# Sixteen expert buffers, the overflow branch behind the last gate and up products, and unpermuted token rows with strided gather columns

## The chip, the cores and the metric

The kernel runs on one core of a Trainium2 chip. The metric is the time of one execution on the device, in microseconds (us). [...] The engines are named as in the views: PE is TensorE's matmul and PEld its weight load, DVE is VectorE, ACT is ScalarE, POOL is GpSimd, SP is SyncE, which here issues nearly all loads.

## The reference, cut to what matters

256 tokens of width 1024 go through two blocks. The change touches only the end of the second one, a mixture of sixteen experts behind a two-level router, and the last norm:

```python
h2_l = modulate(rmsnorm(x_lat, norm2_g[l]), sh2, sc2)
x_lat = x_lat + g2 * hier_moe(h2_l, w_router_group[l], b_router_group[l], w_router_expert[l],
                              b_router_expert[l], w_exp_gate[l], w_exp_up[l], w_exp_down[l])
...
return rmsnorm(x_lat, final_g)

def hier_moe(h, w_rg, b_rg, w_re, b_re, w1, w3, w2):
    ...
    top_v, top_i = lax.top_k(le_g, TOP_K_IN_GROUP)
    w_top = jax.nn.softmax(top_v, axis=-1) * w_grp
    ...
    def expert_step(acc, xs):
        w1e, w3e, w2e, ge = xs
        y = (jax.nn.silu(t @ w1e) * (t @ w3e)) @ w2e
        return acc + ge[:, None] * y, None

    acc, _ = lax.scan(expert_step, jnp.zeros_like(t), (w1, w3, w2, gates))
```

Each token is given two of the four experts of one group. `w1` and `w3` (gate and up) are 1024x512 for each expert and `w2` (down) is 512x1024, all float32: 6 MiB an expert, 96 MiB in all.

## The kernel before

The blocks ahead of the experts take the time up to about 917 us. Then:

**Router.** For each half b of the tokens (128 rows) `x_add(b)` completes the residual `x[b]`, `x_turn(b)` transposes it, `logits(b)` and `pick(b)` give each token its two experts and its rank among the tokens of an expert. `x_high` (ACT, L1707) and `x_low` (DVE, L1711) write the normalized rows as a rounded part and the rest, `xnh` and `xnl` (the tiles H0 to H3). They permute the 1024 columns as they do so (`rows4`, `tiles4`), so that each block of 128 columns in H holds every fourth column of a half of x: this is the order in which a load of expert weights lays its rows on the partitions. The order of these steps on DVE and ACT is that of the code (`route`, a stretch with a manual schedule).

**Slots.** Each expert has 64 slots. `one_hot(b, e0, n)` (DVE, L1772) makes the 0/1 matrix from tokens to slots, first for experts 0 to 3, then for 4 to 15. `gather(p)` (L1788), once for every two pairs of experts, multiplies: for each of eight column blocks k four matmuls (high and low part, two halves of the tokens) with a block of H as the stationary operand, 256 slots as the moving one. The result, half a PSUM bank, is scaled and shifted by DVE into `xe` (L1800). Two consecutive k share a bank. `places()` sums the gates and counts the tokens that found no slot (`novi`).

**Experts.** Two experts form a pair, and TensorE works on both halves of its columns at once (`pair_mm`, 64 columns each). For p = 0 to 7 the program order of TensorE is: `gate(p)`; `down(p-1)` (for p = 0 `places()`); `up(p)`; `gather(p+1)` when p is odd and under 7; `back(p)`, the transposed one-hot; the `add` of pair p-1, which multiplies the slots back into token rows (`scatter`, L1877); `hidden_T(p)`, which transposes the hidden values. Behind the loop come `down(7)`, `scatter(7)` and the last norm (L2015 to L2035).

**Loads.** Each product needs four loads of 1 MiB, 128 partitions by 2048 values, 96 in all. `load_rows` (L235) issues them on SP in program order and takes the buffers in turn from three pools: five `rawa`, four `raw` (these serve the blocks ahead as well), four `rawb`. A load waits until the buffer's last reader is done; SP holds the loads behind it back. So the first thirteen loads (all of gate 0, up 0 and gate 1, and one of down 0) go out ahead of the experts, as their pools' memory comes free.

**Overflow.** Tokens beyond 64 for an expert are treated by a slow path inside `tc.If(nov > 0)` (L1904), in which all engines take part; it isn't taken with this data. Each engine reads `novi` and branches. The branch stands behind `hidden_T(6)`. The loads for `gate(7)`, `down(6)` and `up(7)` are issued in front of it, those for `down(7)` behind it. `down` takes its eight steps (f, n), four blocks f of the hidden columns and two halves n of the output, with f outermost; for p = 7 they are sorted by n, so that the first accumulator is done half-way.

## Time and profile before

| | |
|---|---|
| median of three runs | 1183.94 us (1183.94, 1177.48, 1184.63) |
| the profiled execution's own time | 1180.25 us |
| its span in the trace | 1178.5 us |
| mean granted clock of TensorE | 0.979 |
| PE busy | 1108.8 us (94%) |
| DVE / ACT / POOL busy | 621.2 / 477.3 / 60.7 us |
| instructions | 17991 |

The rows further down come from that one execution; their times are us from the start of its span. "idle before <-" in brackets is the time in which the engine had nothing to do ahead of a row, and the instruction that ended it. A matmul of float32 shows as two records. PEq and SPq are the queues of an engine in which branches, semaphores and DMA issues stand. A DMA share around 1.0 means that the sixteen DMA engines had no pause.

### The profile page before, as it was taken

To read this page: it belongs to the slowest core of one execution; us is meant where nothing else is said; L and a number is where in the kernel's file an instruction comes from. 1 tells how busy PE (TensorE), PEld (TensorE's weight loads), DVE (VectorE), ACT (ScalarE), POOL (GpSimd) and SP (SyncE) were. 2 spreads that over 40 slices of the span, in tenths; PEclk is the share of its full clock that TensorE was granted. 3 is DMA by queue.
4 is the path that set the end of the run, shared out by engine and by line. 5 is a ranking of instruction groups with operands and counts; after the bars stand their busy time and mean duration, and the time that the engine had idled before them with its cause. 6 is when DMAs were issued, how large, how long until landed. Compare 5 with 4: busy or idle time off the path is not lost. (4 is left out here: it accounts for less than half of the span.)

```text
span 1178.5 us, 17991 instructions
## 1 busy us (share of the span) xinstructions
PE 1108.8 (94%) x7527; PEld 870.1 (74%) x7527; DVE 621.2 (53%) x928; ACT 477.3 (40%) x711; POOL 60.7 (5%) x106
## 2 busy tenths in 40 slices
PE   6999999998988999999999999999899799999976
PEld 6999997887756888999998688888898534343432
DVE  4545545556976556455445865666656603232314
ACT  5444444476643355444444445555544300100002
POOL 1000001000330001000000100000000200000000
PEclk9999999999988999999999999999999799999988
DMA  9855654453557548555556454214285399999984
GB/s 338 275 191 179 198 180 158 157 169 112 179 197 261 197 139 304 195 179 185 175 191 218 153 179 160 72 55 152 96 327 210 145 366 419 421 420 420 421 354 175
DMA packets 119538, 262.98 MB, mean 223 GB/s; under 512 B 6873, under 2 KB 83802, under 8 KB 105242
## 3 DMA queue, kind: packets, MB, share of 16 engines
q1 hardware_dynamic: 118506, 258.88, 60.7%
q0 software_dynamic: 656, 2.36, 0.6%
q8 instruction: 61, 1.00, 0.3%
q10 hardware_dynamic: 288, 0.52, 0.1%
q14 instruction: 27, 0.22, 0.1%
HBM read 260.70 MB, written 1.05 MB: 222 GB/s over the span
## 5 line engine op out<-in xcount | busy, mean ns | idle before, releaser
L263 DVE TENSOR_TENSOR lo<-raw,hi 128x1024 fp32r<-128x1024 f32 x243 | 297.2, 1224 | 285.9 <-ACT hi L262 285.5
L262 ACT ACTIVATE hi<-raw 128x1024 fp32r<-128x1024 f32 x246 | 260.6, 1060 | 318.2 <-PE pj L227 203.3
L227 PE MATMUL pj<-H,hi 128*128 128x256 f32 x752 | 212.4, 283 | 4.1 <-issue 4.1
L226 PE MATMUL pj<-H,hi 128*128 128x256 f32 x752 | 216.2, 288 | 0.0
L228 PE MATMUL pj<-H,lo 128*128 128x256 f32 x752 | 212.4, 282 | 0.4 <-POOL lo L263 0.4
L226 PEld LDWEIGHTS pj<-H,hi 128*128 128x128 f32 x752 | 142.8, 190 | 8.5 <-issue 4.5
L228 PEld LDWEIGHTS pj<-H,lo 128*128 128x128 f32 x752 | 143.0, 190 | 5.2 <-issue 4.5
L227 PEld LDWEIGHTS pj<-H,hi 128*128 128x128 f32 x752 | 142.7, 190 | 1.3 <-issue 0.5
L228 PE MATMUL pj<-hTh,lo 128*128 128x256 f32 x352 | 99.4, 283 | 0.1
L227 PE MATMUL pj<-hTl,hi 128*128 128x256 f32 x352 | 99.2, 283 | 0.0
L226 PE MATMUL pj<-hTh,hi 128*128 128x256 f32 x352 | 99.1, 283 | 0.0
L227 PEld LDWEIGHTS pj<-hTl,hi 128*128 128x128 f32 x352 | 67.3, 192 | 1.3 <-DVE hTl L509 0.8
L226 PEld LDWEIGHTS pj<-hTh,hi 128*128 128x128 f32 x352 | 67.2, 192 | 1.2 <-ACT hTh L508 0.8
L228 PEld LDWEIGHTS pj<-hTh,lo 128*128 128x128 f32 x352 | 67.4, 192 | 0.3 <-DVE lo L263 0.3
L1881 DVE TENSOR_TENSOR yf<-yacc,K 128x512 f32<-128x512 f32 x16 | 11.0, 691 | 104.7 <-PE yacc L1832 82.5
L404 PE MATMUL acc<-lo,hTh 128*128 128x512 f32 x160 | 63.1, 394 | 0.0
L403 PE MATMUL acc<-hi,hTh 128*128 128x512 f32 x160 | 62.7, 392 | 0.0
L407 PE MATMUL acc<-hi,hTl 128*128 128x512 f32 x160 | 49.9, 393 | 0.0
L1832 PE MATMUL pu<-rawa,xe 128*64 128x512 f32 x160 | 45.3, 605 | 0.0
L1864 ACT ACTIVATE hT<-eT 128x512 f32<-128x512 f32 x8 | 4.8, 597 | 91.6 <-PE eT L1863 91.6
L1832 PE MATMUL pg<-raw,xe 128*64 128x512 f32 x128 | 35.8, 595 | 0.0
L1832 PE MATMUL yacc<-rawb,hT 128*64 128x512 f32 x128 | 35.5, 592 | 0.0
(496 smaller groups left out, 1895.2 us busy)
## 6 DMA issues: line engine op xcount, KB each, us to landing
raw<-in_w_in_dram SPq DMA_DIRECT2D x43, 1024.0 KB, 5.1
raw<-in_ffn_up_dram SPq DMA_DIRECT2D x22, 1024.0 KB, 5.2
raw<-in_ffn_down_dram SPq DMA_DIRECT2D x22, 1024.0 KB, 4.9
raw<-in_ffn_gate_dram SPq DMA_DIRECT2D x21, 1024.0 KB, 5.2
rawa<-in_w_exp_up_dram SPq DMA_DIRECT2D x20, 1024.0 KB, 19.2
raw<-in_w_exp_gate_dram SPq DMA_DIRECT2D x16, 1024.0 KB, 14.1
rawb<-in_w_exp_down_dram SPq DMA_DIRECT2D x16, 1024.0 KB, 17.5
raw<-in_w_mod_dram SPq DMA_DIRECT2D x15, 1024.0 KB, 5.0
```

What stands on the lines that cost most here:

```text
L226: mm(o, l[0], r[0], start=first, stop=False)
L227: mm(o, l[0], r[1], start=False, stop=False)
L228: mm(o, l[1], r[0], start=False, stop=last)
L262: ACT.activation(hi, r, AF.Copy)
L263: low = lambda: (sub or DVE).tensor_tensor(lo, r, f32(hi), op=OP.subtract)
L403: mm(ps[b][n], hh, wh[:, s_], start=first and f == 0, stop=False)
L404: mm(ps[b][n], hh, wl[:, s_], start=False, stop=False)
L407: mm(ps[b][n], ll, wh[:, s_], start=False, stop=last and f == 1)
L1832: mm(o[halves[u]], l[:, 64 * u:64 * u + 64], r[u], start=first, stop=last, tile_position=(0, 64 * u))
L1864: ACT.activation(t, ps, AF.Copy)
L1881: tt(part(yf, n), yaccs[p][n], part(g2b, n), op=OP.mult)
```

## The change

Seven things are edited together.

- **Buffers.** The expert loads take sixteen buffers in turn: five `rawa`, one that is made of the constant tiles K0 and K1 (now one tile K01), four `raw`, six `rawb`. To make room, the pool "moe" keeps two instead of four general tiles and one `xe` instead of two; `yf` of the scatter lives in K2; the gain of the residual (`g1b`) gets a tile of its own; final_g is loaded into K0 at the end, and the last norm uses K1 and the `xe` tile.
- **Rows.** `x_high` and `x_low` no longer permute; each is one operation on 128x1024. The permutation moves into `gather`, whose stationary operand is now every fourth column of H (a step of 16 bytes).
- **Gather.** The even k are evacuated by DVE, the odd ones by ACT. The first gather takes four banks at once, and both one-hots for experts 4 to 15 stand behind it.
- **Router.** PE joins the manual schedule of `route`.
- **Branch.** It stands behind `hidden_T(7)`; all loads, those of `down(7)` too, are issued in front of it.
- **Last product.** `down(7)` takes f = 0 and 1 for both halves n, then f = 2, 3 of the first half, then of the second.
- **Slow path.** Its loads go to ACT's queue; its tiles change with the pools.

```diff
@@ -98,7 +98,7 @@
     ffn={"4": 16, "2": 11, "1": 2, "m": 12},
     mid={"r4": 9, "r2": 6, "r1": 7, "rm": 16, "v4": 3, "s4": 6, "sm": 6, "gm": 4, "m2": 2, "mm": 2, "pm": 4, "cm": 4, "c1": 2},
     blk={"4": 9, "2": 5, "1": 7, "m": 25}, att={"4": 6, "2": 9},
-    moe={"4": 4, "xe": 2, "oh": 2, "h": 3, "1": 2, "m": 16}, raws=(5, 4, 4))
+    moe={"4": 2, "xe": 1, "oh": 2, "h": 3, "1": 2, "m": 16}, raws=(5, 1, 4, 6))
 
 
 class Stop(Exception):
@@ -238,9 +238,11 @@
         if i < n[0]:
             raw = P["raw1"].tile([128, 2048], F32, name="rawa", tag="rawa", bufs=n[0])
         elif i < n[0] + n[1]:
+            raw = K01
+        elif i < n[0] + n[1] + n[2]:
             raw = raw_tile()
         else:
-            raw = P["raw2"].tile([128, 2048], F32, name="rawb", tag="rawb", bufs=n[2])
+            raw = P["raw2"].tile([128, 2048], F32, name="rawb", tag="rawb", bufs=n[3])
         nraw[0] += 1
         nc.sync.dma_start(raw, src.rearrange("(p k) n -> p (k n)", k=k))
         return raw
@@ -444,7 +446,8 @@
                        channel_multiplier=-1)
 
     H = [cp.tile([128, 1024], F32R, name=f"H{i}") for i in range(4)]
-    K4 = [cp.tile([128, 1024], F32, name=f"K{i}") for i in range(4)]
+    K01 = cp.tile([128, 2048], F32, name="K01")
+    K4 = [K01[:, 0:1024], K01[:, 1024:2048]] + [cp.tile([128, 1024], F32, name=f"K{i}") for i in (2, 3)]
     nhalf = cp.tile([128, 32], F32, name="nhalf")
     POOL.memset(nhalf, -0.5)
     nones = cp.tile([128, 128], F32, name="nones")
@@ -1651,7 +1654,7 @@
     att.close()
     P["raw1"] = es.enter_context(tc.tile_pool(name="raw1", bufs=1, side="right", reuse_waits="tile"))
 
-    g1b, g2b = K4[1], K4[3]
+    g1b, g2b = t4("gb"), K4[3]
     part = lambda t, n: t[:, 512 * n:512 * n + 512]
     for n in range(2):
         ACT.activation(part(g1b, n), mod_bcast(mhl[0], n), AF.Copy)
@@ -1674,7 +1677,7 @@
     L, rsx = cp.tile([128, 2, 20], F32, name="L"), cp.tile([128, 2], F32, name="rsx")
     xnh, xnl, xT = H[0:2], H[2:4], [t4("xT") for _ in range(2)]
     pl = pa("lgp")
-    route = tc.manual_schedule(engines={mybir.EngineType.DVE, mybir.EngineType.Activation})
+    route = tc.manual_schedule(engines={mybir.EngineType.DVE, mybir.EngineType.Activation, mybir.EngineType.PE})
     route.__enter__()
 
     def x_add(b):
@@ -1701,17 +1704,12 @@
                 ACT.activation(part(xT[b], kh), ps, AF.Copy)
 
 
-    rows4 = lambda t: t.rearrange("p (h q j) -> p h j q", h=2, j=4)
-    tiles4 = lambda t: t.rearrange("p (h j q) -> p h j q", h=2, j=4)
 
     def x_high(b):
-        for h in range(2):
-            ACT.activation(tiles4(xnh[b])[:, h], rows4(x[b])[:, h], AF.Copy, scale=rsx[:, b:b + 1])
+        ACT.activation(xnh[b], x[b], AF.Copy, scale=rsx[:, b:b + 1])
 
     def x_low(b):
-        for h in range(2):
-            DVE.scalar_tensor_tensor(tiles4(xnl[b])[:, h], rows4(x[b])[:, h], rsx[:, b:b + 1], tiles4(f32(xnh[b]))[:, h],
-                                     op0=OP.mult, op1=OP.subtract)
+        DVE.scalar_tensor_tensor(xnl[b], x[b], rsx[:, b:b + 1], f32(xnh[b]), op0=OP.mult, op1=OP.subtract)
 
     def logits(b):
         for k in range(8):
@@ -1778,8 +1776,6 @@
         one_hot(b, 0, 4)
     pr16 = big("pr16")
     DVE.tensor_copy(pr16, pr[:, 0:32].rearrange("p (b n) -> p b n", b=2))
-    fg = K4[2]
-    nc.gpsimd.dma_start(fg, bass.AP(tensor=I["final_g_2"].tensor, offset=I["final_g_2"].offset, ap=[[0, 128], [1, D]]))
     gsl = sm("gsl", 8)
     novi = mp.tile([1, 1], I32, name="novi", tag="novi", bufs=1)
     xe, hps, yaccs, hTs, backs = {}, {}, {}, {}, {}
@@ -1790,16 +1786,21 @@
         t = alloc("xe", 2048, "xe", F32, "")
         for u in range(2):
             xe[p + u] = lambda k, u=u: t[:, 256 * k + 128 * u:256 * k + 128 * u + 128]
+        pss = pc2("gat") + pc2("gat") if p == 0 else [None] * 4
         for k in range(8):
-            if k % 2 == 0:
-                ps = pa("gat")
-            o, s_ = ps[:, 256 * (k % 2):256 * (k % 2) + 256], slice(128 * k, 128 * k + 128)
+            ps = pss[k // 2] = pss[k // 2] or pa("gat")
+            o, g = ps[:, 256 * (k % 2):256 * (k % 2) + 256], t[:, 256 * k:256 * k + 256]
             for i, w in enumerate((xnh, xnl)):
                 for b in range(2):
-                    mm(o, w[b][:, s_], oh[b][:, 128 * p:128 * p + 256], start=i + b == 0, stop=i + b == 2)
-            DVE.tensor_scalar(t[:, 256 * k:256 * k + 256], o, sc2p[:, k:k + 1], sh2p[:, k:k + 1], op0=OP.mult, op1=OP.add)
-            if p == 0 and k in (1, 3):
-                one_hot(k // 2, 4, 12)
+                    mm(o, w[b][:, 512 * (k // 4) + k % 4:512 * (k // 4) + 512:4], oh[b][:, 128 * p:128 * p + 256],
+                       start=i + b == 0, stop=i + b == 2)
+            if k % 2:
+                ACT.activation(g, o, AF.Identity, bias=sh2p[:, k:k + 1], scale=sc2p[:, k:k + 1])
+            else:
+                DVE.tensor_scalar(g, o, sc2p[:, k:k + 1], sh2p[:, k:k + 1], op0=OP.mult, op1=OP.add)
+        if p == 0:
+            for b in range(2):
+                one_hot(b, 4, 12)
 
     def places():
 
@@ -1869,14 +1870,14 @@
         raws = ahead.pop((p, 2), None) or fetch(p, 2)
         steps = [(f, n) for f in range(4) for n in range(2)]
         if p == 7:
-            steps.sort(key=lambda v: v[1])
+            steps[4:] = [(2, 0), (3, 0), (2, 1), (3, 1)]
         for f, n in steps:
             o = 1024 * (f % 2) + 512 * n
             pair_mm(yaccs[p][n], hTs[p][:, 128 * f:128 * f + 128], [r[:, o:o + 512] for r in raws[f // 2]], f == 0, f == 3)
 
     def scatter(p):
 
-        yf, yh_, yl_ = t4("yf"), t4("yh", F32R), t4("yl", F32R)
+        yf, yh_, yl_ = K4[2], t4("yh", F32R), t4("yl", F32R)
         for n in range(2):
             tt(part(yf, n), yaccs[p][n], part(g2b, n), op=OP.mult)
             ACT.activation(part(yh_, n), part(yf, n), AF.Copy)
@@ -1897,7 +1898,7 @@
         def some(w, k, i, n):
 
             t = t4("few")
-            nc.sync.dma_start(t.rearrange("p (k n) -> p k n", k=n), w.rearrange("(p k) n -> p k n", k=k)[:, i:i + n])
+            nc.scalar.dma_start(t.rearrange("p (k n) -> p k n", k=n), w.rearrange("(p k) n -> p k n", k=k)[:, i:i + n])
             return t
 
         nov = nc.values_load(novi, min_val=0, max_val=512)
@@ -1905,16 +1906,16 @@
             e_ = mybir.EngineType
             with tc.manual_schedule(engines={e_.PE, e_.DVE, e_.Activation, e_.Pool, e_.SP}):
                 for b in range(2):
-                    t, xT = t4("yf"), t4("yh")
+                    t, xo = K4[2], alloc("xe", 2048, "xo", F32, "")
+                    xT, hp, hT = xo[:, 0:1024], xo[:, 1024:1536], xo[:, 1536:2048]
                     tt(t, f32(xnh[b]), f32(xnl[b]), op=OP.add)
                     for k in range(8):
                         ps = pa("gat")
-                        PE.transpose(ps[:, 0:128], t[:, 128 * k:128 * k + 128], ident)
+                        PE.transpose(ps[:, 0:128], t[:, 512 * (k // 4) + k % 4:512 * (k // 4) + 512:4], ident)
...
@@ -2005,14 +2005,16 @@
             if add:
                 add()
             hTs[p] = hidden_T(hps[p], alloc("h", 512, "hT", F32, ""))
-            if p == 6:
-                ahead.update({k: fetch(*k) for k in ((7, 0), (6, 2), (7, 1))})
+            if p == 7:
+                ahead[7, 2] = fetch(7, 2)
                 overflow()
         down(7)
         scatter(7)()
 
 
-    xn, sq = [t4("xn") for _ in range(2)], t4("sq")
+    fg, sq, xn = K4[0], K4[1], alloc("xe", 2048, "xn", F32, "")
+    nc.gpsimd.dma_start(fg, bass.AP(tensor=I["final_g_2"].tensor, offset=I["final_g_2"].offset, ap=[[0, 128], [1, D]]))
+    xn = [xn[:, 0:1024], xn[:, 1024:2048]]
     rs, ss = [sm("rs", 1) for _ in range(2)], [sm("ss", 2) for _ in range(2)]
     for n in range(2):
         for b in range(2):
```

How it moves instructions, first on SP's queue at the end of the program. Before (L245 is the issue of an expert load, `novi` the count that the branch reads; the slow path's own loads are left out):

```order
L245 DMA raw<-in_w_exp_down_dram 128x2048 x3
L245 DMA rawb<-in_w_exp_down_dram 128x2048
L245 DMA rawb<-in_w_exp_up_dram 128x2048 x3
L245 DMA rawa<-in_w_exp_up_dram 128x2048
L1903 TENSOR_LOAD novi
L1904 COMPARE_AND_BRANCH
...
L1904 UNCONDITIONAL_BRANCH x2
L1903 ISA x2
L245 DMA rawa<-in_w_exp_down_dram 128x2048 x4
L2035 DMA out_dram<-xn 128x512 x2
```

After:

```order
L247 DMA raw<-in_w_exp_up_dram 128x2048 x2
L247 DMA rawb<-in_w_exp_up_dram 128x2048 x2
L247 DMA rawb<-in_w_exp_down_dram 128x2048 x4
L1904 TENSOR_LOAD novi
L1905 COMPARE_AND_BRANCH
L1905 UNCONDITIONAL_BRANCH x2
L1904 ISA x2
L2037 DMA out_dram<-xn 128x512 x2
```

The last four loads, those of `down(7)`, stood behind the branch and stand in front of it now.

Next DVE at the first gather, before (`rank` is the PSUM tile of the ranks, `gat` a gather's bank, `oh` the one-hots):

```order
L1773 TENSOR_TENSOR oh<-c_67,rank 128x256 x2
L1780 COPY pr_8933<-rank 128x32
L1800 TENSOR_SCALAR xe<-gat,sc2p,sh2p 128x256 x2
L1773 TENSOR_TENSOR oh<-c_67,rank 128x768
L1800 TENSOR_SCALAR xe<-gat,sc2p,sh2p 128x256 x2
L1773 TENSOR_TENSOR oh<-c_67,rank 128x768
L1800 TENSOR_SCALAR xe<-gat,sc2p,sh2p 128x256 x4
L1977 RECIPROCAL den<-den 128x2
```

After:

```order
L1736 SCALAR_TENSOR_TENSOR m_8820<-rk,sel 128x16
L1771 TENSOR_TENSOR oh<-c_67,rank 128x256 x2
L1778 COPY pr_8929<-rank 128x32
L1800 TENSOR_SCALAR xe<-gat,sc2p,sh2p 128x256 x4
L1771 TENSOR_TENSOR oh<-c_67,rank 128x768 x2
L1977 RECIPROCAL den<-den 128x2
```

Four of the eight evacuations have left DVE (ACT has them), and the two wide one-hots stand behind the rest.

On PE the same place after the change (`pg` are the matmuls of `gate(0)`; each `gat` row here is one of four matmuls of a column block, on H0 to H3, and blocks 4 and 5 and the last stand alike):

```order
L1795 MATMUL gat<-oh,H_78 128x256
L1795 MATMUL gat<-oh,H_79 128x256
L1795 MATMUL gat<-oh,H_80 128x256
L1795 MATMUL gat<-oh,H_81 128x256
L1833 MATMUL pg<-rawa,xe 64x512
L1795 MATMUL gat<-oh,H_78 128x256
...
L1833 MATMUL pg<-rawa,xe 64x512 x2
L1795 MATMUL gat<-oh,H_78 128x256
...
L1833 MATMUL pg<-rawa,xe 64x512 x11
```

Three blocks come first, then one row of the gate, two blocks, two rows, two blocks, two rows, the last block and the other eleven rows. Before, six blocks came first, then three rows, a block, four rows, the last block and nine rows.

## Rows read from the trace of the kernel before

**Rows 1.** Table of stretches: busy us (instructions) of each engine, granted clock, DMA share.
```profile
core 0: us, PE busy (x) PEld busy (x) DVE busy (x) ACT busy (x) POOL busy (x), PEclk, DMA share, GB/s
919.70:933.30 13.60, 7.32 (x32) 6.77 (x31) 8.94 (x25) 4.37 (x5) 4.21 (x22) 0.50 0.55 227
950.40:953.80 3.40, 3.40 (x12) 0.97 (x10) 0.00 (x0) 0.00 (x0) 0.00 (x0) 0.50 0.99 419
1040.00:1120.00 80.00, 76.37 (x368) 32.59 (x370) 23.69 (x41) 7.28 (x12) 0.00 (x0) 1.00 1.01 421
1127.90:1134.70 6.80, 3.99 (x10) 1.40 (x12) 0.00 (x0) 0.00 (x0) 0.00 (x0) 0.50 1.01 408
```
**Rows 2.** Timeline of SP (start us, us, what is issued): first and last expert loads.
```profile
942.37 4.60 SPq L245 DMA_DIRECT2D rawa<-in_w_exp_down_dram  x3
...
1147.75 2.04 SPq L245 DMA_DIRECT2D rawa<-in_w_exp_down_dram  x4
```
**Rows 3.** Instructions of line 1904, the branch: ns min/median/max, first and last start.
```profile
L1904 SPq EVENT_SEMAPHORE  x8: 17/17/17, 1141.9 to 1147.3; - x8
...
L1904 PEldq COMPARE_BRANCH  x1: 6164/6164/6164, 1124.1 to 1124.1; - x1
L1904 DVEq COMPARE_BRANCH  x1: 72/72/72, 1124.6 to 1124.6; - x1
```
**Rows 4.** Timeline of PE, first gather and gate (start us, us; idle before, releaser).
```profile
929.16 3.76 PE L1799 MATMUL gat<-oh,H 128*128 128x256 f32 x16 [0.60 <-DVE oh L1773]
933.55 0.73 PE L1799 MATMUL gat<-oh,H 128*128 128x256 f32 x4 [0.64 <-DVE xe L1800]
...
942.92 4.51 PE L1832 MATMUL pg<-rawa,xe 128*64 128x512 f32 x18
```
**Rows 5.** Timeline of DVE ahead of and in the first gather.
```profile
924.16 2.14 DVE L1713 SCALAR_TENSOR_TENSOR H<-x,rsx,H 128x512 fp32r<-128x512 f32 x2
...
933.42 0.94 DVE L1773 TENSOR_TENSOR oh<-c,rank 128x768 fp32r<-128x768 f32 x1
```
**Rows 6.** Costliest groups of the page: busy us, mean ns | idle before.
```profile
L263 DVE TENSOR_TENSOR lo<-raw,hi 128x1024 fp32r<-128x1024 f32 x243 | 297.2, 1224 | 285.9 <-ACT hi L262 285.5
...
L1881 DVE TENSOR_TENSOR yf<-yacc,K 128x512 f32<-128x512 f32 x16 | 11.0, 691 | 104.7 <-PE yacc L1832 82.5
...
L1864 ACT ACTIVATE hT<-eT 128x512 f32<-128x512 f32 x8 | 4.8, 597 | 91.6 <-PE eT L1863 91.6
```
**Rows 7.** Timeline of PE, two rounds of the gather of pairs 6 and 7.
```profile
1092.14 1.21 PE L1799 MATMUL gat<-oh,H 128*128 128x256 f32 x8 [0.64 <-DVE xe L1800]
...
1093.99 1.21 PE L1799 MATMUL gat<-oh,H 128*128 128x256 f32 x8 [0.64 <-DVE xe L1800]
```
**Rows 8.** Timeline of PE: transpositions with strided (L657) and contiguous (L1697) stationary columns.
```profile
829.97 0.65 PE L657 MATMUL shp<-ident,brow 128*128 128x128 f32 x4
...
917.01 0.63 PE L1697 MATMUL trp<-ident,x 128*128 128x128 f32 x4 [0.29 <-DVE x L1686]
```
**Rows 9.** Timeline of PE, from `down(5)` to the end of `down(7)`.
```profile
1107.81 3.60 PE L1832 MATMUL yacc<-raw,hT 128*64 128x512 f32 x16
1111.25 3.60 PE L1832 MATMUL yacc<-rawb,hT 128*64 128x512 f32 x16
...
1130.71 6.04 PE L1832 MATMUL pg<-rawa,xe 128*64 128x512 f32 x17 [6.30 <-PEq L1904]
...
1139.59 4.03 PE L1832 MATMUL yacc<-raw,hT 128*64 128x512 f32 x17
...
1155.57 0.63 PE L1863 MATMUL eT<-ident,hp 128*128 128x128 f32 x4
1156.88 2.79 PE L1832 MATMUL yacc<-rawa,hT 128*64 128x512 f32 x10 [0.69 <-ACT hT L1864]
1160.13 5.36 PE L1832 MATMUL yacc<-rawa,hT 128*64 128x512 f32 x22 [0.46 <-DMA rawa<-in_w_exp_down_dram]
```
**Rows 10.** Groups by line and form, weight loads of PE, 936 to 1166 us.
```profile
L1832 PEld LDWEIGHTS pu<-rawa,xe 128*64 128x64 f32 x160 | 14.0, 139 | 24.5 <-issue 23.0 <-DMA rawa<-in_w_exp_up_dram 0.9 <-PE yacc L1832 0.6
```

More of the change, by code (lines that the diff above doesn't have):

```diff
@@ L1916, in overflow @@
                     for e in range(16):
-                        hp = part(t4("hp"), 0)
                         for i in range(2):
@@ L1927, in overflow @@
                                 ACT.activation(hp, ps, AF.Silu)
-                        hT = hidden_T(hp, part(t4("hT"), 0))
+                        hidden_T(hp, hT)
                         for f in range(4):
@@ L1932, in overflow @@
                                 mm(acc[n], hT[:, 128 * f:128 * f + 128], part(raw, n), start=e + f == 0, stop=e == 15 and f == 3)
-                    t = t4("yf")
                     for n in range(2):
```

## The prediction, made before the changed kernel was run

> **What bounds the kernel now.** The page first: of a span of 1178.5 us the profiled execution spends its last quarter in the sixteen experts, and every line of the change that does work lies behind 917 us. Next the table of stretches [rows 1]: the reader is to see two things. In the middle of the experts (1040 to 1120 us) TensorE is busy 76.37 of 80 us and the DMA engines are busy all the time at 421 GB/s, so neither has room; a 1 MiB load costs 1.0486 MB / 421 GB/s = 2.49 us. [...]
>
> Who waits for whom is then read from the queue of SP [rows 2]. The first load after the thirteen that were fetched early goes out at 942.37 us, as `gate(0)` sets buffers free. Seventy-nine loads later the last one ahead of the branch has landed at 1147.3 (the last of the eight semaphores in [rows 3]): 204.9 us, 2.594 us each, close to the 2.49 of a busy DMA. TensorE waits for a load only twice: 0.9 us in one `up` [rows 10] and 0.46 us in `down(7)` [rows 9]. So TensorE's own chain from the first gather to the last product sets the end, with the DMA a few us ahead of it; time comes off only where this chain has holes. Its holes are the start (929.16 to 947.43, [rows 4]), the branch of the overflow test (6.30 us of idle, then the slow clock, [rows 9]) and the end (0.69 for hT, 0.46 for the load, a slow `down(7)`).
>
> **The change, part by part** (against the profiled execution's 1180.25 us).
>
> *a. `x_low(1)`.* Two operations that read with a stride of four take 2.14 us together, directly ahead of `pick(1)` and so of the rank, the one-hot and the first gather [rows 5]. One contiguous operation on 128x1024 is nearest to the split's 1224 ns [rows 6]. The logits are in by then, and the next operations stand right behind on DVE. **-0.9.** `x_high` shortens as well, on an engine that is not waited for at that point.
>
> *b. `gather(0)` with `gate(0)`.* Before: 929.16 to 942.92 + 4.51 = 947.43, 18.3 us [rows 4]. DVE evacuates all eight tiles and makes two one-hots of 0.94 us between them [rows 5]; TensorE waits for it three times, 0.64 us the first time. Now ACT takes the odd tiles, the one-hots stand behind, and four banks are held. By the new order [the fences above]: one tile of four matmuls at the slow clock (3.76 us for 16 gives 0.85 with the pipeline's lead taken off), evacuation and signals about 1.15, so 2.0; each later round is eight matmuls plus the evacuation of the even tile, for which the odd tile of the same bank still waits. A round at the slow clock is 1.7 + 0.9 = 2.6; at the full clock [rows 7] it takes 1093.99 - 1092.14 = 1.85. With the clock back about 4 us after the gather's start, as before, that is 2.0 + 2.6 + 2 x 1.85, and 0.5 for the last four matmuls: 8.8 us. Five of `gate(0)`'s sixteen pairs of matmuls stand inside the rounds, where TensorE would wait; eleven are left, each two matmuls of the 32 that take 7.04 us in a `down` [rows 9], by twos 0.43 us: 4.7. Sum 13.5 instead of 18.3: **-4.7**. Bounds: nothing (the third rival) and -6.4, if `up(0)` also loses its slow stretch at 950.4 [rows 1].
>
> *c. Strided columns.* No gather of before reads its stationary columns with a stride. The nearest row is the transposition of `brow`, whose stationary columns lie four apart: four take 0.65 us, four contiguous ones 0.63 [rows 8]. A gather's matmuls follow each other faster: 0.117 us (1.21 us for eight, less the 0.27 of the last one's tail) against 0.158 there. So the bound above is 0.158 - 0.117 = 0.041 us for each of the 96 matmuls of the later gathers, +3.9; below it is nothing, as a stride can't speed a load. I take the difference of the two rows, 0.02 / 4 x 128: **+0.6**. [...]
>
> The later gathers (2, 4, 6) gain nothing else: their period of 1.85 us is eight matmuls and the wait of 0.64 for the even tile [rows 7], and that wait stays. ACT's odd tiles hide under the next four matmuls (if not, some 0.2 us a round, 12 rounds, 2.4).
>
> *d. Sixteen buffers.* The loads start when `gate(0)`'s first half is done, now about 938.3 instead of 942.37 (8 pairs, 3.4 us, ahead of 941.8), and three buffers more are full then. The wait in `up` goes: **-0.9**. Eighty loads are left; at 2.49 the last lands at 938.3 + 199.2 + 2.4 of transit = 1140, at the rate of before, 2.594, at 1145.8.
>
> *e. The branch.* Its instructions are the same, and TensorE's row of it is 6164 ns, DVE's 72 [rows 3]. From the transpositions ahead of it to the first matmul behind it TensorE takes 0.63 + 6.30 = 6.93 us [rows 9], and then `gate(7)` takes 1139.59 - 1130.71 = 8.88 instead of 7.04. Behind `hidden_T(7)` it is still on TensorE's path; `down(7)` pays the slow clock instead of `gate(7)`: **0**. It would cost 7 us less with the branch free.
>
> *f. The end.* `fetch(7, 2)` stood behind SP's branch: SP waited there for all loads (1141.9 to 1147.3, [rows 3]), issued four loads from 1147.75 on [rows 2], and `down(7)` took 1156.88 to 1165.49, 8.61 us instead of 7.04. These loads now go out in order ahead of the branch: **-1.6**. The 0.69 us for hT [rows 9] lies under the branch: **-0.7**. SP's wait for all loads now ends at 1140 to 1146, ahead of TensorE's return.
>
> *g. The tail.* With the new order of `down(7)` the first accumulator ends two steps (1.7 us) ahead of the second instead of four; DVE's 0.69, ACT's 0.60 and DVE's 0.69 [rows 6], 1.98 us with no signal counted, no longer fit in between, and the second product starts late: **+0.4**.
>
> *At nothing:* the single `xe` buffer (the first evacuation of a gather stands behind `up(p)`'s last product in any case; without that cover 0.6 us, three times); yh and yl in two buffers (their last reader is the `add` one pair earlier, over 20 us before); the early load into K01 (its last reader is a product of the attention block, and even in the router's stretch the DMA is busy only 0.55, [rows 1]); final_g, 512 KB or 1.25 us of DMA, needed only behind 1160.
>
> Sum: -0.9 - 4.7 + 0.6 - 0.9 - 1.6 - 0.7 + 0.4 = -7.8, so 1172.4 on the profiled execution's scale. In steps: `hidden_T(7)` begins at 1155.57 - 5.9 (a to d) - 8.2 (branch and slow clock, now behind it) = 1141.5; `down(7)` at 1148.4; it ends at 1157.3 instead of 1165.49. The profiled execution is 3.7 us below the median of the three runs (1183.94); the mean of all four is 1181.6, 1.3 above it. I add that: **1173.7 us**.
>
> **Rivals.**
> 1. *As summed*, 1173.7, with 1169 to 1179 from the bounds of c (+3.3), of the slow stretch (-1.7) and the spread of the four times around their mean (1177.48 to 1184.63, some 3 to 4). Chance 0.48.
> 2. *The branch gets shorter.* TensorE's 6.16 us fall in a stretch in which the DMA engines are busy all the time at 408 GB/s [rows 1], and DVE pays almost nothing for the same branch; if TensorE waits for something that stands behind the loads, it waits less once the loads are nearly through (1140 to 1146 against 1141.5). Half of it is -3, and without the slow stretch in `up(0)` -1.7: 1169. It can't go below about 1166 at the loads' rate of before: 1145.8, half a `down` (3.5), the 14.8 from `down(7)`'s end to the end (1180.25 - 1165.49), g's 0.4 and the 1.3 make 1165.8. Against it: the loads end no earlier than the branch begins. Chance 0.22.
> 3. *The first gather gets no shorter*: the odd tile's wait in its bank and the slow clock eat b. Then 1173.7 + 4.7 = 1178.4. For it: each round has the same wait as the later gathers; against it: the two one-hots of 0.94 are gone from DVE's chain. Chance 0.18.
> 4. *Slower: the strided weight loads are exposed.* If a gather's load doubles, a matmul takes 0.235 instead of 0.117 us at the full clock: a round of eight gets 0.9 longer, +3.7 for each of three gathers and about +5 in the first, in place of c's 0.6: 1173.7 + 15.5 = 1189. It turns the sign from 7.8 / 128 = 0.061 us a matmul on. For it: ACT pays double for the stride in `x_high`; against it: [rows 8], which allow 0.041. Chance 0.12.
>
> **How the numbers follow.** The likeliest is the first. A range of 1166 to 1182 leaves out the fourth rival and a little at the lower end: 0.83 is held. A measurement of this kernel can tell about 1% from no change. Faster by over 1% of 1183.94 means under 1172.1: nearly all of the second rival (0.20) and the lower part of the first (0.14), 0.34. Slower by over 1%, over 1195.8, is the part of the fourth with more than a doubling: 0.05. The rest, 0.61, is within 1%.
>
> **What would show it.** The first load after the pause near 938 (d); `gate(0)`'s last matmul near 941.7 and no slow stretch in it (b); a gather's eight matmuls still 1.21 us (c; at 2.1 the fourth rival holds); the branch's row on TensorE still near 6.2 us, and the granted clock 0.5 at the start of `down(7)` (e; a row near 3 is the second rival); no gap in SP's issues ahead of the last four loads, and no wait in `down(7)` (f). The forecast is wrong if TensorE waits for loads in pairs 5 to 7: then the DMA has become the bound and its 80 loads set the end.

## The result, and the profile after

The changed kernel takes 1192.62 us (median of six runs, 1190.68 to 1198.01); the kernel before takes 1181.52 (six runs, 1177.48 to 1184.63). The ratio is 1.0102, with a 95% interval of 1.0076 to 1.0129: slower by 1%, where 1173.7 was forecast, and outside the range of 1166 to 1182. The fourth rival has come true. (The ratios here are the recorded estimates with their intervals; they differ by up to 0.0015 from the quotient of the medians. Beside the experiments the kernel before was measured again, with medians of 1181.58, 1181.63 and 1181.66 us.)

The profiled execution (1198.01 us, span 1196.3) is the longest of the six, and 6.3 us of the difference to the one of before lie ahead of all that the change touches but the early loads: the first transposition of the router starts at 921.54 us, in the kernel before at 915.25. In the other ten traces of this study it starts between 916.15 and 921.41. The granted clock of the earlier blocks differs between the two executions: up to that transposition its mean is 0.98 here and 0.99 in the one of before, over the first 300 us 0.98 and 1.00. The changed kernel with a step of eight (experiment 2) has the same early loads and starts at 916.15. So stages are compared from that transposition on; a table with all kernels stands behind the experiments.

First the gather's instructions (ns as minimum/median/maximum), which answer to the gather of [rows 7]: the weight loads of the kernel before, then loads and matmuls after (line 1795):

```profile
L1799 PEld LDWEIGHTS gat<-oh,H x128: 186/188/338, 929.1 to 1098.0; 128*128 128x128 f32 x128
```
```profile
L1795 PEld LDWEIGHTS gat<-oh,H x128: 308/330/337, 934.6 to 1118.1; 128*128 128x128 f32 x128
L1795 PE MATMUL gat<-oh,H x128: 392/437/604, 934.6 to 1118.3; 128*128 128x256 f32 x128
```

The median weight load of a gather takes 330 ns instead of 188. What that does is seen in the timeline of PE, gather of pairs 6 and 7 (start, us, idle before in brackets):

```profile
1106.97 1.21 PE L1795 MATMUL gat<-oh,H 128*128 128x256 f32 x4
1108.82 2.24 PE L1795 MATMUL gat<-oh,H 128*128 128x256 f32 x8 [0.64 <-DVE xe L1800]
1111.69 2.26 PE L1795 MATMUL gat<-oh,H 128*128 128x256 f32 x8 [0.64 <-DVE xe L1800]
1114.59 2.23 PE L1795 MATMUL gat<-oh,H 128*128 128x256 f32 x8 [0.64 <-DVE xe L1800]
1117.46 1.31 PE L1795 MATMUL gat<-oh,H 128*128 128x256 f32 x4 [0.64 <-DVE xe L1800]
1118.57 0.63 PE L1827 MATMUL oht<-ident,oh 128*128 128x128 f32 x2
1118.85 0.78 PE L1890 MATMUL scat<-yh,back 128*128 128x512 f32 x1
```

A round takes 1114.59 - 1111.69 = 2.90 us where it took 1.85 [rows 7]; the wait of 0.64 in it is the same. The table of stretches for the same gather (columns as in [rows 1]; PEclk, the granted clock, is called full at 1.00 and slow at 0.50):

```profile
1107.00:1110.00 3.00, 2.36 (x11) 2.16 (x10) 1.29 (x2) 0.00 (x0) 0.00 (x0) 1.00 1.01 418
1110.00:1113.40 3.40, 2.76 (x12) 2.47 (x12) 0.54 (x1) 0.92 (x2) 0.00 (x0) 0.54 1.02 424
1113.40:1120.20 6.80, 5.52 (x20) 4.73 (x20) 1.62 (x4) 1.33 (x3) 0.00 (x0) 0.50 1.00 416
```

Eight matmuls take 2.24 us in the round of 1108.82, most of which lies at the full clock, and 2.23 in that of 1114.59, all of it at the slow one: 0.23 us a matmul at either level. Contiguous matmuls take 0.117 us at the full clock. At the slow one they take 0.213: so far apart are the first sixteen of the first gather in the kernel before (3.76 us for all, [rows 4]), and the median of their contiguous loads is 330 ns too. So the stride doubles the time from one matmul to the next at the full clock (0.117 to 0.234 us), and adds only 0.02 us at the slow one. And the clock falls to 0.50 in the gather, which it didn't before, so that the scatter behind it runs slowly too (its weight loads take 259 and 251 ns on the mean up to there, 188 in the kernel before).

The end, as the timeline of PE and the instructions of line 1905 (the branch) show it; they answer to [rows 3, 9]:

```profile
1168.46 0.63 PE L1864 MATMUL eT<-ident,hp 128*128 128x128 f32 x4
1173.16 9.75 PE L1833 MATMUL yacc<-rawb,hT 128*64 128x512 f32 x32 [4.07 <-PEq L1905]
```
```profile
L1905 SPq EVENT_SEMAPHORE  x8: 17/17/17, 1145.0 to 1160.4; - x8
...
L1905 PEldq COMPARE_BRANCH  x1: 4084/4084/4084, 1168.8 to 1168.8; - x1
```

The branch on TensorE is 2.1 us shorter than before, all loads had landed 8 us ahead of it (1160.4), and no product waits for a load any more. `down(7)` takes 9.75 us instead of 7.04 with the granted clock at 0.50 from 1173.1 to 1177.0. SP issues the last four loads at 1139.53, 3.4 us behind the two ahead of them and behind no branch, which answers to [rows 2]:

```profile
1136.10 0.80 SPq L247 DMA_DIRECT2D rawb<-in_w_exp_up_dram  x2
1139.53 4.24 SPq L247 DMA_DIRECT2D rawb<-in_w_exp_down_dram  x4
```

Of the prediction's signs, the one for c came out as the fourth rival's (over 2.1 us for eight matmuls), and the branch's row lies between those of e and the second rival (4.1, where 6.2 and 3 were named). The sign for d failed: the first load after the pause goes out at 949.30, which is 943.0 counted from the first transposition as in the trace before; there it went out at 942.37, and 938 was said.

### The profile page after: what moved, and what is told of

It is laid out like the page before. It is cut to its first block, busy times and chain, and to the rows that moved or that the text cites. A ratio compares the mean times of both kernels' runs of the same rounds, so it can differ in the third digit from the quotient of the medians.

```text
span 1196.3 us, 18004 instructions
## 1 busy us (share of the span) xinstructions
PE 1132.2 (95%) x7527; PEld 892.4 (75%) x7527; DVE 612.9 (51%) x910; ACT 484.0 (40%) x725; POOL 59.7 (5%) x106
## 3 DMA queue, kind: packets, MB, share of 16 engines
q0 software_dynamic: 656, 2.36, 0.5%
## 5 line engine op out<-in xcount | busy, mean ns | idle before, releaser
L264 ACT ACTIVATE hi<-raw 128x1024 fp32r<-128x1024 f32 x246 | 260.6, 1060 | 323.3 <-PE pj L227 207.7
L227 PE MATMUL pj<-H,hi 128*128 128x256 f32 x752 | 214.7, 286 | 4.5 <-issue 4.5
L226 PE MATMUL pj<-H,hi 128*128 128x256 f32 x752 | 218.5, 291 | 0.0
L226 PEld LDWEIGHTS pj<-H,hi 128*128 128x128 f32 x752 | 145.3, 193 | 8.6 <-issue 4.7
L227 PEld LDWEIGHTS pj<-H,hi 128*128 128x128 f32 x752 | 145.2, 193 | 1.3 <-issue 0.5
L1882 DVE TENSOR_TENSOR K<-yacc,K 128x512 f32<-128x512 f32 x16 | 11.1, 691 | 101.0 <-PE yacc L1833 101.0
L1795 PE MATMUL gat<-oh,H 128*128 128x256 f32 x128 | 36.9, 447 | 8.9 <-DVE xe L1800 8.3
L1795 PEld LDWEIGHTS gat<-oh,H 128*128 128x128 f32 x128 | 31.6, 328 | 18.1 <-DVE xe L1800 13.4
L1798 ACT ACTIVATE xe<-gat,sh2p,sc2p 128x256 f32<-128x256 f32 x16 | 9.0, 564 | 66.4 <-PE gat L1795 66.4
L409 PEld LDWEIGHTS acc<-hi,hTl 128*128 128x128 f32 x160 | 30.1, 188 | 6.9
## 6 DMA issues: line engine op xcount, KB each, us to landing
rawa<-in_w_exp_gate_dram SPq DMA_DIRECT2D x14, 1024.0 KB, 13.9
rawb<-in_w_exp_up_dram SPq DMA_DIRECT2D x12, 1024.0 KB, 13.1
```

What stands on the lines that cost most here:

```text
L226: mm(o, l[0], r[0], start=first, stop=False)
L227: mm(o, l[0], r[1], start=False, stop=False)
L264: ACT.activation(hi, r, AF.Copy)
L409: mm(ps[b][n], ll, wh[:, s_], start=False, stop=last and f == 1)
L1795: mm(o, w[b][:, 512 * (k // 4) + k % 4:512 * (k // 4) + 512:4], oh[b][:, 128 * p:128 * p + 256], start=i + b == 0, stop=i + b == 2)
L1798: ACT.activation(g, o, AF.Identity, bias=sh2p[:, k:k + 1], scale=sc2p[:, k:k + 1])
```

## The experiments

**1. The stride undone, the stride alone.** ("Run 1" below is the first of these two, the contiguous one.) The question was whether the loss is the strided weight load, or the new order and evacuations of the gather. The first kernel takes the stride out of the changed one, the second puts it into the kernel before.

```diff
-        ACT.activation(xnh[b], x[b], AF.Copy, scale=rsx[:, b:b + 1])
+        for h in range(2):
+            ACT.activation(tiles4(xnh[b])[:, h], rows4(x[b])[:, h], AF.Copy, scale=rsx[:, b:b + 1])
...
-                    mm(o, w[b][:, 512 * (k // 4) + k % 4:512 * (k // 4) + 512:4], oh[b][:, 128 * p:128 * p + 256],
+                    mm(o, w[b][:, 128 * k:128 * k + 128], oh[b][:, 128 * p:128 * p + 256],
```

> The changed kernel with one part undone: x_high and x_low permute the rows again, and the gather's stationary columns are contiguous. All else stays (sixteen buffers, branch behind hidden_T(7), four banks, ACT's half of the evacuations). Stride theory: the changed kernel shows 0.234 us from one gather matmul to the next, at the full clock and at the slow one, and a weight load of 330 ns; the time is lost there and in the slow clock that follows. Then the spacing goes back to 0.117 us, the load to 188 ns, gathers of pairs 2, 4 and 6 take 7.4 us instead of 11.3 (3 x 3.9 = 11.8), the scatter behind them runs at the full clock (some 5), the first gather with its gate takes 13.5 instead of 18.8 (5.3), x_low costs 0.9 more: 1192.6 - 21 = 1171 to 1173. Rival, the order and the evacuations: the loss comes from the odd tiles on ACT, the single xe tile and the new order around the first gather. Then the gathers keep a round of about 2.9 us and the time stays at 1188 to 1193.

Measured: 1173.99 us, just above the 1171 to 1173 expected; ratio to the kernel before 0.9933 (0.9909 to 0.9957). The loads are back at 188 ns:

```profile
L1801 PEld LDWEIGHTS gat<-oh,H x128: 186/188/333, 932.9 to 1098.7; 128*128 128x128 f32 x128
```

and a stretch over the gather of pairs 6 and 7 keeps the full clock:

```profile
1091.40:1099.00 7.60, 5.02 (x35) 4.20 (x34) 2.83 (x5) 1.70 (x3) 0.00 (x0) 1.00 1.01 418
```

The second kernel is the same edit the other way round, in the kernel before.

> The kernel before with that one part alone: unpermuted rows (one x_high and one x_low for each half) and gather columns with a step of four; thirteen buffers, branch behind hidden_T(6), all evacuations on DVE. Stride theory: gathers of pairs 2, 4 and 6 take 11.3 instead of 7.4 us each (11.8), the slow clock behind them costs up to 5 more, the first gather some 2, x_low gives 0.9 back: 1181.5 + 18 = 1199, at least 1193. Rival (order and evacuations): within 1 us of 1181.5.

Measured: 1194.41 us, ratio 1.0113 (1.0067 to 1.0159): over the 1193 expected at least, short of the sum of 1199. Its loads, with thirteen buffers and all evacuations on DVE:

```profile
L1793 PEld LDWEIGHTS gat<-oh,H x128: 307/329/339, 928.2 to 1110.8; 128*128 128x128 f32 x128
```

So the stride costs 18.6 us in the changed kernel (1192.62 - 1173.99) and 12.9 in the kernel before (1194.41 - 1181.52), in both with what x_low gives back in it. The table of stages below shows where the two differ: in the kernel before, pairs and first gather get 14.0 us longer, but the router 2.0 and the end 1.5 shorter. The order and the evacuations have no part in the loss.

**2. Which stride.** Columns two apart (8 bytes) and eight apart (32 bytes), in the changed kernel; the diff is of the first.

```diff
+    rows2 = lambda t, a: t.rearrange("p (m a c) -> p a m c", a=2, c=2)[:, a]
+    tiles2 = lambda t, a: t[:, 512 * a:512 * a + 512].rearrange("p (m c) -> p m c", c=2)
...
-                    mm(o, w[b][:, 512 * (k // 4) + k % 4:512 * (k // 4) + 512:4], oh[b][:, 128 * p:128 * p + 256],
+                    mm(o, w[b][:, 512 * (k % 4 // 2) + 256 * (k // 4) + k % 2:512 * (k % 4 // 2) + 256 * (k // 4) + 256:2], oh[b][:, 128 * p:128 * p + 256],
```

> The changed kernel with a step of two (8 bytes) in place of four in the gather's stationary columns: x_high and x_low permute only by pairs, in two operations each. [...] Step theory: any step other than one doubles the load, since the transposition of the hidden values, with a step of two, had loads of 205 ns against 141 for contiguous ones, nearly as long as the 212 of step four: load 315 to 330 ns, spacing 0.22 to 0.234, time 1189 to 1194.

> The changed kernel with a step of eight values (32 bytes) instead of four in the gather's stationary columns; x_high and x_low write runs of four, in two operations each. [...] Distance theory (the cost grows with the step, as 188, 196, 330 ns for one, two and four might also be read): load over 400 ns, spacing 0.3 or more, over 1200.

Measured: with two 1174.53 us (0.9941, 0.9921 to 0.9962), not to be told from the 1173.99 of run 1 and far under the 1189 to 1194 of the step theory; with eight 1191.13 (1.0085, 1.0054 to 1.0117), close to the 1192.62 with four and under the 1200 of the distance theory. The gather's loads, step two and then step eight:

```profile
L1801 PEld LDWEIGHTS gat<-oh,H x128: 192/196/333, 930.9 to 1096.2; 128*128 128x128 f32 x128
```
```profile
L1801 PEld LDWEIGHTS gat<-oh,H x128: 312/338/346, 928.3 to 1110.7; 128*128 128x128 f32 x128
```

188, 196, 330 and 338 ns for steps of one, two, four and eight; at the full clock the matmuls follow each other in 0.117, 0.12, 0.234 and 0.24 us. The step of two costs next to nothing, that of four doubles the time of a matmul, and that of eight adds hardly more. The step theory (315 to 330 ns at two) and the distance theory (over 400 at eight) have fallen. The runs place the doubling between steps of 8 and 16 bytes; no step between them was run, and why it lies there no run shows.

**3. Buffers and branch.** Thirteen buffers in the kernel of run 1; the branch alone in the kernel before; and, without a diff here, the second edit backwards in the kernel of run 1.

```diff
-    moe={"4": 2, "xe": 1, "oh": 2, "h": 3, "1": 2, "m": 16}, raws=(5, 1, 4, 6))
+    moe={"4": 2, "xe": 1, "oh": 2, "h": 3, "1": 2, "m": 16}, raws=(5, 0, 4, 4))
```

> The run with contiguous columns (1174.0) with thirteen expert buffers instead of sixteen: K01 is not used for loads and rawb has four. Theory of the lead: TensorE never waited for a load with sixteen, and the last one landed at 1151.4 on that trace, only 0.5 us ahead of the first product behind the branch. With thirteen, 83 instead of 80 loads are left after the pause, 3 x 2.5 = 7.5 us more for the DMA: the last load lands near 1158 and down(7) waits for it, 2 to 4 us on the path, and the 0.9 in one up is back: 1177 to 1179. Rival (what the prediction said, term d): only the 0.9 comes back: 1175.

```diff
-            if p == 6:
-                ahead.update({k: fetch(*k) for k in ((7, 0), (6, 2), (7, 1))})
+            if p == 7:
+                ahead[7, 2] = fetch(7, 2)
                 overflow()
```

> The kernel before with the branch part alone: it stands behind hidden_T(7), and fetch(7, 2) in front of it; thirteen buffers. Theory of the shorter branch (its row on TensorE is 6.2 us while the DMA is full and 3.3 to 4.1 with the loads through, as in the four runs so far): the branch 2 to 3 less, hT's wait 0.7 less, the load's late issue gone; but with thirteen buffers the last load lands at 1147.3 + 4 x 2.5 = 1157, so down(7) can't end before about 1160.5 instead of 1165.5: -5, 1176.5. Theory of the prediction (terms e and f, the branch keeps its 6.9 us and the slow clock): -2.3, 1179.

> The run with contiguous columns (sixteen buffers, 1174.0) with the branch back behind hidden_T(6) and the loads of down(7) behind it, as in the kernel before. (Two small tiles of the slow path lie elsewhere, since the single xe tile is still in use there.) It completes a square: thirteen buffers and branch late 1180.4, thirteen and early 1180.4. Theory of the pair (buffers and late branch pay only together: the early branch costs its 6.2 us while the DMA is full, and in that hole the loads catch up anyway): the branch 2.9 longer than the 3.3 there, hT's wait of 0.7 back, sometimes a slow gate(7): 1177 to 1180. Rival (the buffers alone bring the gain): 1174 to 1175.

Measured: thirteen with the late branch 1180.41 (0.9983, 0.9966 to 1.0001), 1.4 us above what the theory of the lead gave; the branch alone 1182.77 (0.9996, 0.9980 to 1.0011); sixteen with the early branch 1179.24 (0.9967, 0.9948 to 0.9986), as the theory of the pair said. The fourth corner, thirteen and early with the new gather, is the run of 4 below, 1180.43; it keeps the pools and the order of `down(7)` of the kernel before, so that the square is closed but for these.

| | branch behind hidden_T(6) | behind hidden_T(7) |
|---|---|---|
| thirteen buffers | 1180.43 | 1180.41 |
| sixteen buffers | 1179.24 | 1173.99 |

Either part alone is worth at most about 1 us, which these intervals can't tell from nothing; both together 6.4, which they can. Why the branch alone brings nothing is in the timeline of PE of that kernel (the branch alone in the kernel before):

```profile
1139.98 0.64 PE L1832 MATMUL yacc<-rawb,hT 128*64 128x512 f32 x1 [1.19 <-DMA rawb<-in_w_exp_down_dram]
...
1145.06 3.65 PE L1832 MATMUL pu<-rawb,xe 128*64 128x512 f32 x16 [1.42 <-DMA rawb<-in_w_exp_up_dram]
...
1150.02 0.64 PE L1832 MATMUL pu<-rawa,xe 128*64 128x512 f32 x1 [1.30 <-SPq L1904]
...
1160.08 1.97 PE L1832 MATMUL yacc<-rawa,hT 128*64 128x512 f32 x4 [3.72 <-PEq L1904]
```

In `down(6)` and `up(7)` TensorE now waits for loads, which it didn't do in the kernel before (the wait laid to the branch's line in `up(7)` ends with a load too: the `rawa` of that product lands at 1150.0). The early branch had been a hole of 6.3 us in which the loads caught up. Moved away, it leaves a wait in its place, 1.19 + 1.42 + 1.30 = 3.9 us, and costs its 3.7 us again later. Only with three loads fewer behind the pause, 7.5 us of DMA at 2.49 us a load, does the hole really go: in the two kernels with sixteen buffers no matmul behind the first pair waits for a load, with the branch early or late. Both theories of the branch alone expected a gain, and both missed.

**4. The gather's part alone**, in the kernel before.

```diff
+        pss = pc2("gat") + pc2("gat") if p == 0 else [None] * 4
...
+            if k % 2:
+                ACT.activation(g, o, AF.Identity, bias=sh2p[:, k:k + 1], scale=sc2p[:, k:k + 1])
```

> The kernel before with the gather's part alone: ACT evacuates the odd column blocks, the first gather takes four banks, both wide one-hots stand behind it, PE joins the manual schedule; columns contiguous, rows permuted. By the prediction (term b) the first gather with its gate takes 13.5 instead of 18.3 us: -4.7, 1176.8. By the run with contiguous columns, whose first gather and gate took 16.15 us (932.93 to 949.08): -2.1, 1179.4. Gathers 2, 4 and 6 unchanged at 7.4 us in both.

Measured: 1180.43 us, 0.9987 (0.9966 to 1.0008): no change that can be told, and above both expectations. In its trace the first gather and gate take 16.3 us. But in the trace of the kernel with the branch alone, whose gather is that of before, they take 16.6, against 18.3 in the kernel before. The table of stretches tells the three executions' difference; the kernel before, then the branch alone:

```profile
929.10:933.30 4.20, 3.76 (x16) 3.49 (x16) 1.23 (x4) 1.50 (x2) 3.17 (x17) 0.50 0.00 0
933.30:936.80 3.50, 2.02 (x12) 1.34 (x13) 2.67 (x5) 0.00 (x0) 0.00 (x0) 0.99 0.00 0
936.80:940.20 3.40, 3.40 (x10) 1.16 (x6) 0.70 (x2) 0.00 (x0) 0.00 (x0) 0.51 0.00 0
```
```profile
933.90:938.00 4.10, 3.75 (x16) 3.49 (x16) 1.14 (x4) 1.50 (x2) 3.16 (x17) 0.50 0.00 0
938.00:942.00 4.00, 2.44 (x13) 1.45 (x14) 3.17 (x6) 0.00 (x0) 0.00 (x0) 0.97 0.00 0
942.00:950.60 8.60, 8.60 (x39) 3.04 (x36) 1.92 (x5) 0.00 (x0) 1.26 (x7) 1.00 0.49 157
```

The same instructions fell into a second slow stretch (936.8 to 940.2) in one execution and not in the other. Of the 18.3 us from which term b started, 1.6 were that.

**5. The branch last, and a version from all this.** Run 1 with the branch behind `scatter(7)`; then step two, the branch last, and xn in a load buffer.

```diff
-            if p == 7:
-                ahead[7, 2] = fetch(7, 2)
-                overflow()
         down(7)
         scatter(7)()
+        overflow()
```

> The same as the run with contiguous columns, with the branch moved once more: behind scatter(7), where TensorE has nothing left to do. Theory of the branch (its row on TensorE, 4.1 us in the changed kernel, and the slow clock of down(7) behind it, 9.75 us instead of 7.04, lie on the path): 4.1 + 2.7 = 6.8 us less, of which the tail gives back about 1, since DVE and ACT can no longer interleave the last norm with the last additions: 1165 to 1167 where the contiguous run gives 1172. Rival: the loads set the end (the last one lands near 1145 to 1150 on the trace's scale): then it gains less than 3.

> A candidate from the runs so far: the changed kernel with a column step of two, the branch behind scatter(7), and the last norm's xn in a load buffer instead of the xe tile, which the slow path uses on TensorE. In the run with the branch last, DVE waited 2.85 us for TensorE's branch before it began xn. Theory of the tile (it waited because the slow path's TensorE reads that tile): the wait goes, and x_high and x_low gain another 0.7: 1171.3 - 2.85 - 0.7 = 1168. Rival (the wait belongs to the end of the branch itself, where the engines meet): 1171.

Measured: 1171.30 (0.9898, 0.9852 to 0.9945) and 1169.73 (0.9891, 0.9863 to 0.9919). Both fell short of what was expected. The first gained 2.7 instead of 5 to 7 against run 1, and the two intervals overlap, so even that isn't clear (by the stages it is 0.5): `down(7)` of run 1 had lost nothing to the clock (7.09 us), its branch was only 3.3 long, and DVE waited for TensorE's branch in the tail. In the second this wait is gone, 0.65 instead of 2.85, by DVE's timeline of the two:

```profile
1164.86 1.90 DVE L2027 TENSOR_TENSOR xn<-x,K 128x512 f32<-128x512 f32 x3 [2.85 <-PEq L1911]
```
```profile
1160.82 1.90 DVE L2027 TENSOR_TENSOR rawa<-x,K 128x512 f32<-128x512 f32 x3 [0.65 <-DVEq L1911]
```

So the shared tile was its cause; of these 2.2 us the tail got 1.2 shorter (15.6 to 14.4), since DVE then waits twice for POOL's factors (0.87 and 0.83). The last version is 1.0% faster than the kernel before and 1.9% faster than the changed one.

**The stages of all kernels**, us, each from one trace by the starts and ends of PE's rows: first transposition of the router to first gather; to the end of `gate(0)`; to `hidden_T(7)`; to the end of `down(7)`; to the end of the span.

| kernel | router | gather(0), gate(0) | pairs | end | tail | sum |
|---|---|---|---|---|---|---|
| before | 13.9 | 18.3 | 208.1 | 9.9 | 13.0 | 263.3 |
| changed | 13.1 | 18.9 | 214.9 | 14.5 | 13.4 | 274.7 |
| 1 contiguous | 13.2 | 16.1 | 198.9 | 11.1 | 13.4 | 252.6 |
| 1 stride in before | 11.9 | 19.8 | 220.6 | 8.4 | 13.1 | 273.8 |
| 2 step two | 13.3 | 17.2 | 197.3 | 13.2 | 13.4 | 254.3 |
| 2 step eight | 12.2 | 19.0 | 215.1 | 12.8 | 13.4 | 272.5 |
| 3 thirteen, late | 13.8 | 17.1 | 203.6 | 11.0 | 13.4 | 258.8 |
| 3 branch in before | 13.9 | 16.6 | 205.1 | 13.1 | 13.0 | 261.8 |
| 3 sixteen, early | 13.4 | 15.9 | 207.7 | 8.5 | 14.0 | 259.5 |
| 4 gather in before | 13.0 | 16.3 | 207.9 | 10.2 | 13.0 | 260.4 |
| 5 branch last | 13.5 | 15.8 | 198.8 | 8.4 | 15.6 | 252.1 |
| 5 last version | 13.3 | 17.2 | 197.3 | 8.4 | 14.4 | 250.5 |

The early branch counts under "pairs", the late one under "end". An "end" of 11.1 and one of 13.2 differ by a slow stretch in `down(7)` (7.09 and 8.78 us), which comes and goes. By the stages the change costs 11.4 us, by the medians 11.1.

## Why the prediction was wrong, step by step

**c, the strided columns, is the step that failed.** It gave +0.6 for all 128 matmuls, and +3.9 as the bound for the 96 of the later gathers; the runs show +18.6, net of what a gives back (0.9 was said for a). What failed is the transfer from one kind of matmul to another: c took the pace of a transposition for that of a gather. The loads' own rows in the trace of the kernel before, strided and contiguous:

```profile
L657 PEld LDWEIGHTS shp<-ident,brow x8: 195/212/218, 829.9 to 835.4; 128*128 128x128 f32 x8
```
```profile
L1697 PEld LDWEIGHTS trp<-ident,x x16: 138/140/143, 915.0 to 917.3; 128*128 128x128 f32 x16
```

A transposition's load gets half as long again with the stride, from 140 to 212 ns, and its matmuls still follow each other in 0.12 us, against 0.11; the pace hides what the load lost. A gather's load goes from 188 to 330, and its pace from 0.117 to 0.234. The bound of 0.041 us had a slip besides: for the gather the last matmul's tail was taken off (0.117), for the transpositions it was not (0.63 / 4 = 0.158). With the tail off the strided ones take (0.65 - 0.28) / 3 = 0.12 us, a gather's pace, so the bound mended would have been near nothing, and further off. Loads that are half as long again would have called for more than 0.12 on the fourth rival.

Of the 22.1 us between the stages of the changed kernel and of the contiguous one, the pairs hold 16.1: three gathers of 11.6 instead of 7.5 us (12.1), and the slow clock behind them (from the gather's end to the next gate 3.6 to 4.6 us instead of 2.6; 4.0). The rest is gather(0) with 2.8, and 3.4 in the branch and `down(7)`, the latter a slow stretch that some executions have.

The fourth rival had the mechanism, the strided load exposed, and nearly the price: 3.7 us for each of three gathers (4.0 measured) and 5 for the first (2.8). Twelve of the first gather's 32 matmuls run at the slow clock in run 1, where the stride costs 0.02 us each, and the other 20 lose 0.117: 2.6 us by this estimate. Its sign from ACT is in both traces: `x_high` takes 1204 ns for 512 permuted columns before and 1147 ns for 1024 unpermuted ones after. What the rival lacked was the slow clock behind the later gathers (4.0), and a chance above 0.12.

**The rest of the sum came out at 1174.0, by luck: its errors cancel.** Without c, and without a, which run 1 leaves out, it is 1173.7 - 0.6 + 0.9 = 1174.0; run 1 measured 1173.99. By the corners of the square, b is worth 1.2 us (4.7 was said), d and g with the early branch 1.2 (0.5), and e and f, with sixteen buffers, 5.2 (2.3); neither 1.2 is clear of the noise. Of the terms:
- *a* held: `x_low(1)` takes 1.28 us instead of 2.14.
- *b* said -4.7. Run 4 gives -4.0 to +0.9 by its interval, and the first gather and gate take 15.8 to 17.1 us in the five traces with the new order and contiguous columns, 16.6 and 18.3 in the two of the old one. The base held a slow stretch; and the gate's matmuls inside the rounds don't hide under the waits: in run 1 a full-clock round with two of them takes 942.04 - 939.88 = 2.16 us, not 1.85.
- *d* fits by itself: with three loads fewer behind the pause no `up` waits any more, and in run 1 they start at 944.86, on the scale of the trace before 940.4, so 2.0 us earlier, where 4.1 was said. What it missed is that it decides what the late branch is worth: from thirteen to sixteen buffers it is 6.4 us there, not 0.9.
- *e* said 0; the late branch is 2 to 3 us shorter on TensorE, as the second rival had it. With thirteen buffers that gains nothing, because the old place was a hole that the loads needed; with sixteen, e and f give 5.2 instead of 2.3.
- *f* held: no wait for hT, and no wait for a load. The lead is less than the changed kernel shows (8 us): there the slow gathers gave the loads time. In run 1 the last one landed at 1151.4, half a us ahead of the first product of `down(7)`.
- *g* held: the tail takes 13.4 instead of 13.0.

## What to carry to other kernels

Where a stationary operand gets a stride, look at the weight load's own duration, not at the pace of the matmuls over it, and don't take it from another kind of matmul: where no row of the same kind has the stride, its cost is open until it is run. In this gather a step of two float32 values (8 bytes) was all but free (0.12 us a matmul at the full clock, 0.117 contiguous), and a step of four (16 bytes) doubled the time of a matmul (0.234). A stall that is moved must be checked for what used it: here loads caught up behind a branch, and only more buffers made its removal count (5.2 us with sixteen, nothing that can be told with thirteen). And a base taken from one execution should be checked for slow stretches of the clock before a term is subtracted from it.

## What the runs showed of the hardware

- The gather's matmuls with strided loads (step four) follow each other in 0.234 us at the granted clock 1.00 and in 0.233 to 0.239 at 0.50: the same pace at both. With contiguous loads it is 0.117 at 1.00 and 0.213 at 0.50.
- The granted clock fell to 0.50 in all nine gathers of the pairs behind the first in the three kernels with a step of four or eight (in the changed one at about 990.8, 1052.3 and 1110.3 us), and in none of the 27 in the other nine. Ahead of the fall at 1110.3 in the changed kernel PE was busy 2.36 of 3.00 us; it stayed at 1.00 in a contiguous gather with PE busy 5.02 of 7.60, and in the products of [rows 1] with 76.37 of 80. The busy time of the records doesn't tell the two apart, and what makes the clock fall no run shows.
- The transpositions don't follow the gather's pattern: their loads take 140 ns contiguous, 205 with a step of two (line 1863 of the kernel before) and 212 with four, but the gather's 188, 196 and 330. Why stays open.
- The branch takes TensorE 6.0 to 6.2 us in the four kernels that have it behind `hidden_T(6)`, with the DMA busy all the time there, and 3.3 to 4.1 in the eight that have it later, with a DMA share of 0.04 to 0.48. Among these eight the time doesn't follow the share (4.1 at 0.04, 3.3 at 0.48). Place and DMA load changed together, so no run shows which of them the longer time comes from.
